# Hymba-style layer on one core: the last row tile first in the routing, two token tiles and three gate units between the embedding's steps

## Chip, core and metric
One core of one Trainium2 chip. The time is the device time of one execution in microseconds (us), as the median of runs. Engines: PE (TensorE), DVE (VectorE), ACT (ScalarE), POOL (GpSimd), SP (SyncE, which here issues most DMAs).

## What is computed
One decoder layer over 1024 tokens of width 1024 in fp32: a mixer (retention and mLSTM heads) with its output projection, a mixture of 32 experts, a gated embedding per layer, and a final norm.
```python
xn = rms_norm(h, attn_norm[l])
h = h + mixer(xn, ...)
xn = rms_norm(h, moe_norm[l])
h = h + hier_moe(xn, ...)      # best group of 4, then 2 of its 8 experts, SwiGLU
...                            # then h gets the gated embedding:
e = rms_norm(p @ w_ple_up, ple_norm)
h = h + sigmoid(rms_norm(h, ple_gate_norm) @ w_ple_gate) * e
```
The routing takes, per token, logits of 4 groups and 32 experts from the normalised row, chooses two experts, sorts the tokens by expert and gathers each expert's rows.

## The kernel before
**Products.** Every large product is three fp32r matmuls (mm3, L216-220): high x high, low x high, high x low. So each operand is split into a high part (a copy on ACT, rounded) and a low part (DVE: value minus high part). Weights come as *units* of 128x2048 (1 MB). The class that streams them has `fetch_to` (SP issues the DMA into a ring of raw buffers as soon as one is free), `split_to` (splits the units up to a number) and `get(u, look)` (gives unit u and splits up to `look` units ahead). Units in `pool_low` have their low part made by POOL (L147), as one 2048-wide operation; units with a scale, as the four of the gate, are split in four pieces by L136 (ACT) and L137 (DVE). A raw buffer is free again when both parts are made.

**Order.** The kernel is scheduled by hand: the order in which the program issues is the order on each engine. Side work is kept in generators that the main loops advance (`pump`, `drain`, `next`).

**Output projection and routing.** Rows are in 8 tiles of 128. `out_half(1, ...)` (L1001 and around) makes rows 512 to 1023 in two column halves. For a finished tile t, `square` (ACT), `norm` (POOL and DVE), `h_trans(t, c)` (4 transposes and a copy to `zT`, by DVE L913 for c = 1), `h_scale` (multiplication L944 and a store into `g_dram`, which the experts gather from) and `last_logits` (4 narrow matmuls L922, then DVE L933 adds the two column halves and L934 scales them) follow. When the last product is done, the kernel drains the side work, issues fetches, then takes the logits of tile 6 (`last_b(6)`), squares, norms and transposes of tile 7 (`last_a(7)`), then tile 7's logits. The routing `route(4)` is a long chain of small DVE operations (from L1247) with a few matmuls (L1263, L1285, L1329) and ends with the gathers of the first experts (POOL L1343). While it runs, units m0+2 and m0+3 (m0: first expert unit) are split with `pool_low`, and m0+4 at the head of `moe`.

**Experts.** A loop over 32 experts: transpose the gathered rows, w1, w3, SiLU, w2; from some expert on one step of the embedding per expert is put between. `gemm2` copies its result, scaled, by ACT (L1394) and scatters it by POOL (L1395) to `Y_dram`. In the last expert's `gemm2`, `look` splits ahead: gate units 0 and 1.

**Branch.** `overflow()` (L1484, L1485) loads a count into every engine and skips a loop that serves experts with too many tokens; in these inputs it is not taken.

**Tail.** The embedding generator `ple` has a step for each tile and column half, here called t2c0 to t7c1 behind the branch: 6 matmuls, a square with a sum by ACT (L1167), and after the second half the reciprocal root on POOL (L1169, L232, L233). In the step c = 0 of tile j the operand of tile j+1 is split (`tps`), and the scaling of tile j-1 (DVE L1146) frees its two accumulators; there are four accumulators. `fill(n)` advances it by n steps; the last `next` only scales tile 7. `add(t)` (DVE L1626, four operations) adds the two experts' rows from `Y_dram`; `trans(t)` (L1635 on) transposes the sum, splits it into `gth` (ACT L236) and `gtl` (DVE L237) and squares it on ACT (L1639). `first(t)` is the gate product of tile t's first column half with gate units 0 and 1, its Sigmoid (ACT L1665, with the load of its function table) and the sums. The second half takes units 2 and 3. From the second row tile on, all tiles repeat one pattern.

Of the kernel before, what the change touches and what calls it, by code (L numbers as in the profile page):

```python
# [10 lines left out]
F32 = mybir.dt.float32  # L11
# [11 lines left out]
P = 128  # L23
# [6 lines left out]
NE = 32  # L30
# [149 lines left out]
class Layer:  # L180
# [674 lines left out]
    def outproj(self):  # L855
# [83 lines left out]
        def h_scale(half, c, n):  # L939

            t, s = half * 4 + n, slice(c * 512, c * 512 + 512)
            hg = post.tile([P, 512], F32, name="hg", bufs=2)
            eng = v if half and c else nc.gpsimd
            eng.tensor_tensor(hg, hb[half, c][:, n], gm[:, s], op=OP.mult)  # L944
            nc.sync.dma_start(self.g_dram[t * P:(t + 1) * P, s], hg)

        def h_store(half, c):
            nc.sync.dma_start(rows(self.h_dram, half, c), hb[half, c])
# [25 lines left out]
        def out_half(half, pumps, before, after):  # L974
            nonlocal y67
            for c in range(2):
                if half == 0 and c == 1:
                    y67 = hold.tile([P, 2, D], F32, name="y67", tag="hb", bufs=3)
                    loaded = {}
                if c:  # L980
                    self.side.append(first_columns(half * 4))
                accs = [psA.tile([P, 512], F32, name="acc") for _ in range(4)]
                _, _, units = self.oplan[half * 2 + c]
                pace = pumps["out%d" % c]
                for ui, u in enumerate(units):
                    H, L = W.get(u, 2 if half and c and ui else 1)
                    for n in range(4):
                        s = slice(n * P, n * P + P)
                        if c == 0 and ui == 0 and n == 0:
                            self.late_last(half * 4)  # L990
                            if half:
                                x_again(1, 0)
                        before(c, ui, n)
                        for kk in range(4):
                            k = ui * 4 + kk
                            self.mm3(accs[n], XH[:, k, s], XL[:, k, s], H[:, kk, :], L[:, kk, :], k == 0, k == KD - 1)
                            if kk == 1:
                                self.pump(pace / 2)
                        if ui == 1:
                            v.tensor_tensor(hb[half, c][:, n], accs[n], hb[half, c][:, n], op=OP.add)  # L1000
                            h_scale(half, c, n)  # L1001
                            if n == 3:
                                h_store(half, c)
                        after(c, ui, n)
                        if half:
                            W.fetch_to(W.nf + 2)
                        if half == 0 and c == 1:
                            j = ui * 4 + n
                            for t in range(4, NT):
                                if t not in loaded and (t, 0) in self.y_done and (t, 1) in self.y_done:  # L1010
                                    self.y_load(t)
                                    loaded[t] = j
                            if j >= 5:
                                self.y_trans(j - 1)
                        self.pump(pace / 2)
                self.mark("out %d %d" % (half, c))
# [17 lines left out]
        def last_a(t):  # L1034
            square(t, 1)
            norm(t)
            h_trans(t, 1)

        last_b = last_logits
        out_half(1, self.PACE[1], none, after)  # L1040
        self.drain()
        self.late_slots = 2
        W.ahead = 99
        W.fetch_to(W.nf + 1)
        last_b(6)
        last_a(7)
        last_b(7)
        ctxP.close()
        pair = self.xp.tile([P, 2 * DX], F32, name="xt", bufs=1)
        nc.gpsimd.memset(pair[:, D:DX], 0.0)  # L1050
# [3 lines left out]
        W.halves = self.m0 + self.HV  # L1054
        W.fetch_to(W.nf + 1)
        next(r)
        W.pool_low = (self.m0 + 2, self.m0 + 3)
        W.split_to(self.m0 + 3)
        for _ in range(4):
            next(r)  # L1060
        for _ in r:
            pass

# [285 lines left out]
    def moe(self):  # L1349
# [52 lines left out]
        hs = {}  # L1402
        blocks = self.overflow_list()
        gather(1)
        W.split_to(self.m0 + 4)
        norm_x(0)
        trans_x(0)
        for e in range(NE + 1):
# [30 lines left out]
        self.tail_open()  # L1439

    def look(self, e, which):
        return 3 if e < self.LK else 2


# [153 lines left out]
    def tail(self):  # L1598
# [21 lines left out]
        def add(t):  # L1620
            h = self.th[t]
            y0, y1 = ty[t]
            for c in range(2):
                for y in (y0, y1):
                    s = slice(c * 512, c * 512 + 512)
                    v.tensor_tensor(h[:, s], h[:, s], y[:, s], op=OP.add)  # L1626

        def trans(t):
            h = self.th[t]
            th = tq.tile([P, KD, P], F32R, name="gth")  # L1630
            tl = tq.tile([P, KD, P], F32R, name="gtl")
            for b in range(2):
                p = psB.tile([P, 4, P], F32, name="pb")
                for k in range(4):
                    nc.tensor.transpose(p[:, k, :], h[:, (4 * b + k) * P:(4 * b + k + 1) * P], self.ident)  # L1635
                self.split_pair(th[:, 4 * b:4 * b + 4], tl[:, 4 * b:4 * b + 4], p)
            gt[t] = (th, tl)
            st = rs[t] = tq.tile([P, 2], F32, name="tst")
            nc.scalar.activation(ty[t][1], h, AF.Square, accum_out=st[:, 0:1])  # L1639
            self.rstd(st[:, 1:2], st[:, 0:1], D)  # L1640
# [45 lines left out]
        def fill(n):  # L1686
            for _ in range(n):
                next(self.ple_gen, None)
# [4 lines left out]
        self.tail_load(1)  # L1693
        load(0)
        load(1)
        fill(9)
        add(0)
        fill(2)
        self.ctxE.close()
        tq = ctxQ.enter_context(tc.tile_pool(name="tq", bufs=2, side="right", reuse_waits="tile"))  # L1700
        self.fn = self.tp.tile([P, D], F32, name="tpt")
        trans(0)
        fill(2)
        add(1)
        self.tail_load(2)
        load(2)
        nc.sync.dma_start(self.fn, bcast_rows(i["final_norm"], D))
# [3 lines left out]
        def first(t, mid=None):  # L1711
            acc = accs[t] = psA.tile([P, 512], F32, name="acc")
            gemm(t, 0, acc, mid=mid)
            finish(t, 0, acc)
# [12 lines left out]
        for t in range(NT):  # L1727
            acc = [None, None]
            if not t:
                first(0, lambda: trans(1))  # L1730
                W.ahead = 99
                W.split_to(len(W.units))
                first(1)
                add(2)
            elif t > 1:
                first(t)
            if t:
                following(t)
            acc[1] = psA.tile([P, 512], F32, name="acc")
            if t < NT - 1:  # L1740
                gemm(t, 1, acc[1])
                finish(t, 1, acc[1])
            else:
                for a, s in ((acc[1], slice(0, 256)), (psA.tile([P, 512], F32, name="acc"), slice(256, 512))):
                    gemm(t, 1, a, s)
                    finish(t, 1, a, s)
            self.mark("gate %d" % t)
            if 2 < t + 2 < NT:
                add(t + 2)
# [52 lines left out]
```

## Time and profile before
| what | value |
|---|---|
| runs | 1323.55 us median of 3 (1320.59 to 1325.12) |
| profiled execution | 1325.77 us, its span 1324.0 us |
| busy | PE 1276.4 us (96%), DVE 948.4 (72%), ACT 787.7 (59%), POOL 289.7 (22%) |
| mean granted TensorE clock | 0.984 |
| stages, us from the span's start | mixer to some 480, projection to 572, routing to 597, experts to 1185, branch to 1189, embedding steps and first additions to 1211, gate to 1324 |

All times in rows are from the start of the span. Matmul rows overlap: the distance of their starts is what one costs. The number in brackets is the idle time of that engine just before, and what released it; "DVEq" is VectorE's sequencer.

### The profile page before, as it was taken

The page shows a single profiled execution, that of the slowest core. Times are in us where ns is not written, and L with a number is a line of the kernel's source. Part 1 is how long each engine was busy: PE and PEld are TensorE (multiplying, and loading weights), DVE is VectorE, ACT ScalarE, POOL GpSimd, SP SyncE. Part 2 cuts the span into 40 slices and gives each one's busy share as a digit, 9 for nine tenths or more (in the row PEclk, how much of TensorE's full clock was granted, in tenths as well). Part 3 has the DMA queues.
Part 4 walks back from the last instruction along what each step waited for, and adds up shares of the span by engine and source line. Part 5 has one row for each costly group of instructions (what it writes and reads, how often), then busy time and mean ns, then how long its engine had stood idle before and what let it go on. Part 6 is the DMA issues. An engine that isn't in the chain of part 4 may idle for free. (4 is left out here: it accounts for less than half of the span.)

```text
span 1324.0 us, 17536 instructions
## 1 busy us (share of the span) xinstructions
PE 1276.4 (96%) x6408; PEld 1061.2 (80%) x6408; DVE 948.4 (72%) x1327; ACT 787.7 (59%) x1154; POOL 289.7 (22%) x364
## 2 busy tenths in 40 slices
PE   7999999999999999959999999999999999988997
PEld 7987888988888888747888888888888887876786
DVE  4557645347773535877999889999999998885665
ACT  5744343434443334336888878888888888774533
POOL 1053112215120442131111121111111231012232
PEclk9999999999999999979999999999999999999999
DMA  9323331332324356857999999999999589956421
GB/s 347 134 98 111 108 121 62 106 110 89 113 88 175 128 212 254 344 202 260 364 387 371 356 376 374 376 368 378 375 375 384 209 358 395 344 191 240 159 96 64
DMA packets 62141, 317.76 MB, mean 240 GB/s; under 512 B 11763, under 2 KB 12339, under 8 KB 32484
## 3 DMA queue, kind: packets, MB, share of 16 engines
q1 hardware_dynamic: 48196, 284.75, 57.4%
q0 software_dynamic: 13712, 31.84, 6.6%
q8 instruction: 51, 0.84, 0.2%
q14 instruction: 38, 0.31, 0.1%
q10 hardware_dynamic: 144, 0.04, 0.0%
HBM read 299.83 MB, written 33.65 MB: 252 GB/s over the span
## 5 line engine op out<-in xcount | busy, mean ns | idle before, releaser
L218 PE MATMUL acc<-wh,XH 128*128 128x512 f32 (+2 forms) x544 | 211.2, 388 | 7.6 <-ACT wh L145 7.2
L219 PE MATMUL acc<-wl,XH 128*128 128x512 f32 (+2 forms) x544 | 203.9, 375 | 1.1 <-DVE wl L147 1.1
L220 PE MATMUL acc<-wh,XL 128*128 128x512 f32 (+2 forms) x544 | 203.9, 375 | 0.3 <-DVE XL L349 0.3
L147 DVE TENSOR_TENSOR wl<-raw,wh 128x1024 fp32r<-128x1024 f32 (+4 forms) x85 | 128.6, 1536 | 77.4 <-ACT wh L145 77.4
L1395 POOL DMA_INDIRECT Y_dram<-y,idx_s x32 | 44.9, 1403 | 471.2 <-ACT y L1394 450.6
L145 ACT ACTIVATE wh<-raw 128x1024 fp32r<-128x1024 f32 (+4 forms) x86 | 110.5, 1314 | 48.3 <-PE acc L220 29.4
L218 PEld LDWEIGHTS acc<-wh,XH 128*128 128x128 f32 x544 | 103.7, 191 | 24.9 <-ACT wh L145 7.4
L220 PEld LDWEIGHTS acc<-wh,XL 128*128 128x128 f32 x544 | 103.5, 190 | 18.2 <-DVE XL L349 0.5
L219 PEld LDWEIGHTS acc<-wl,XH 128*128 128x128 f32 x544 | 103.9, 191 | 17.2 <-DVE wl L147 1.6
L218 PE MATMUL acc<-XH,xth 128*128 128x512 f32 x256 | 104.7, 409 | 0.4 <-ACT xth L236 0.4
L220 PE MATMUL acc<-XH,xtl 128*128 128x512 f32 x256 | 101.5, 396 | 0.3 <-DVE xtl L237 0.3
L219 PE MATMUL acc<-wl,xth 128*128 128x512 f32 x256 | 101.5, 397 | 0.0
L219 PE MATMUL acc<-XL,xth 128*128 128x512 f32 x256 | 101.5, 397 | 0.0
L220 PE MATMUL acc<-wh,xtl 128*128 128x512 f32 x256 | 101.5, 397 | 0.0
L218 PE MATMUL acc<-wh,xth 128*128 128x512 f32 x256 | 101.0, 394 | 0.0
L147 DVE TENSOR_TENSOR XL<-raw,XH 128x1024 fp32r<-128x1024 f32 x58 | 68.3, 1219 | 15.9 <-ACT XH L145 15.9
L147 DVE TENSOR_TENSOR wl<-rawB,wh 128x1024 fp32r<-128x1024 f32 (+1 forms) x61 | 72.9, 1235 | 2.1 <-ACT wh L145 2.1
L147 DVE TENSOR_TENSOR XL<-rawB,XH 128x1024 fp32r<-128x1024 f32 x48 | 56.6, 1218 | 8.4 <-ACT XH L145 8.4
L145 ACT ACTIVATE wh<-rawB 128x1024 fp32r<-128x1024 f32 (+1 forms) x61 | 61.9, 1067 | 0.0
L147 DVE TENSOR_TENSOR XL<-rawH,XH 128x1024 fp32r<-128x1024 f32 x48 | 56.5, 1219 | 7.1 <-ACT XH L145 7.1
L147 DVE TENSOR_TENSOR wl<-rawH,wh 128x1024 fp32r<-128x1024 f32 x48 | 56.5, 1218 | 4.8 <-ACT wh L145 4.8
L220 PEld LDWEIGHTS acc<-XH,xtl 128*128 128x128 f32 x256 | 48.9, 191 | 11.7 <-DVE xtl L237 1.0
(417 smaller groups left out, 3113.5 us busy)
## 6 DMA issues: line engine op xcount, KB each, us to landing
rawB<-in_w SPq DMA_DIRECT2D x56, 1024.0 KB, 8.5
raw<-in_w SPq DMA_DIRECT2D x53, 1024.0 KB, 8.3
rawH<-in_w SPq DMA_DIRECT2D x48, 1024.0 KB, 8.1
hb<-in_w SPq DMA_DIRECT2D x34, 1024.0 KB, 8.4
raw<-in_w_in SPq DMA_DIRECT2D x24, 1024.0 KB, 4.9
raw<-in_w_out SPq DMA_DIRECT2D x8, 1024.0 KB, 5.0
raw<-in_w_in SPq DMA_DIRECT2D x8, 768.0 KB, 6.9
xl<-in_x SPq DMA_DIRECT2D x4, 1024.0 KB, 8.8
```

The source lines that it names most:

```text
L145: self.nc.scalar.activation(h[:, s], r[:, s], AF.Copy)
L147: low.tensor_tensor(l[:, s], r[:, s], h[:, s].bitcast(F32), op=OP.subtract)
L218: self.lastmm = mm(out, lh, rh, start=first, stop=False)
L219: mm(out, lh, rl, start=False, stop=False)
L220: mm(out, ll, rh, start=False, stop=last)
L1395: st = nc.gpsimd.indirect_dma_start(out=self.Y_dram, out_offset=bass.IndirectOffsetOnAxis(ap=self.idx_s[:, e:e + 1], axis=0), in_=y, in_of ...
```

## The change
It has three parts. In the routing, tile 7's copy of transposes, square, norm and row multiplication are issued before the logits of tiles 6 and 7, and the stores behind. The early splits of m0+2 to m0+4 are taken out; these units are now split where the first expert's products ask for them, with DVE for the low parts. And in the tail, gate units 0 and 1 are split between steps of the embedding instead of before the branch, unit 2 before the first gate product; both tiles' additions and transposes stand between the steps, and a Sigmoid of one element, which takes the table load with it, stands behind tile 0's transposes.
```diff
@@ -998,9 +998,10 @@
                                 self.pump(pace / 2)
                         if ui == 1:
                             v.tensor_tensor(hb[half, c][:, n], accs[n], hb[half, c][:, n], op=OP.add)
-                            h_scale(half, c, n)
-                            if n == 3:
-                                h_store(half, c)
+                            if not (half and c and n == 3):
+                                h_scale(half, c, n)
+                                if n == 3:
+                                    h_store(half, c)
                         after(c, ui, n)
                         if half:
                             W.fetch_to(W.nf + 2)
@@ -1038,13 +1039,20 @@
 
         last_b = last_logits
         out_half(1, self.PACE[1], none, after)
+
+        while (7, 0) not in zT:
+            self.pump(1)
+        h_trans(7, 1)
+        square(7, 1)
+        norm(7)
+        h_scale(1, 1, 3)
         self.drain()
+        last_b(6)
+        last_b(7)
+        h_store(1, 1)
         self.late_slots = 2
         W.ahead = 99
         W.fetch_to(W.nf + 1)
-        last_b(6)
-        last_a(7)
-        last_b(7)
         ctxP.close()
         pair = self.xp.tile([P, 2 * DX], F32, name="xt", bufs=1)
         nc.gpsimd.memset(pair[:, D:DX], 0.0)
@@ -1054,10 +1062,6 @@
         W.halves = self.m0 + self.HV
         W.fetch_to(W.nf + 1)
         next(r)
-        W.pool_low = (self.m0 + 2, self.m0 + 3)
-        W.split_to(self.m0 + 3)
-        for _ in range(4):
-            next(r)
         for _ in r:
             pass
 
@@ -1402,7 +1406,6 @@
         hs = {}
         blocks = self.overflow_list()
         gather(1)
-        W.split_to(self.m0 + 4)
         norm_x(0)
         trans_x(0)
         for e in range(NE + 1):
@@ -1439,6 +1442,8 @@
         self.tail_open()
 
     def look(self, e, which):
+        if which == 2 and e == NE - 1:
+            return 0
         return 3 if e < self.LK else 2
 
 
@@ -1693,15 +1698,24 @@
         self.tail_load(1)
         load(0)
         load(1)
-        fill(9)
+        fill(2)
+        W.split_to(self.gate_units[0] + 1)
+        fill(2)
+        W.split_to(self.gate_units[1] + 1)
+        fill(3)
         add(0)
-        fill(2)
+        fill(1)
+        add(1)
+        fill(1)
         self.ctxE.close()
         tq = ctxQ.enter_context(tc.tile_pool(name="tq", bufs=2, side="right", reuse_waits="tile"))
         self.fn = self.tp.tile([P, D], F32, name="tpt")
         trans(0)
-        fill(2)
-        add(1)
+        sg = tq.tile([P, 1], F32, name="sg", bufs=1)
+        nc.scalar.activation(sg, self.ones[:, 0:1], AF.Sigmoid)
+        fill(1)
+        trans(1)
+        fill(3)
         self.tail_load(2)
         load(2)
         nc.sync.dma_start(self.fn, bcast_rows(i["final_norm"], D))
@@ -1727,7 +1741,8 @@
         for t in range(NT):
             acc = [None, None]
             if not t:
-                first(0, lambda: trans(1))
+                W.split_to(self.gate_units[2] + 1)
+                first(0)
                 W.ahead = 99
                 W.split_to(len(W.units))
                 first(1)
```
In the routing, on DVE, from the last addition of the projection to the routing's first reduction. `LG` are logits, `zT` a copied transpose, `hg` the multiplied rows, `zst` the norm's sums. Before:
```order
L933 TENSOR_TENSOR LG<-lg_4658,pb 128x36
L934 SCALAR_TENSOR_TENSOR LG<-LG,zst,bgr 128x36
L899 TENSOR_TENSOR zst<-zst 128x1
L913 COPY zT<-pb 128x512
L928 COPY lg_4658<-pb 128x36 x2
L933 TENSOR_TENSOR LG<-lg_4658,pb 128x36
L934 SCALAR_TENSOR_TENSOR LG<-LG,zst,bgr 128x36
L899 TENSOR_TENSOR zst<-zst 128x1
L913 COPY zT<-pb 128x512
L933 TENSOR_TENSOR LG<-lg_4658,pb 128x36
L934 SCALAR_TENSOR_TENSOR LG<-LG,zst,bgr 128x36
L1247 TENSOR_REDUCE G_4804<-LG 128x16
```
and with the change:
```order
L899 TENSOR_TENSOR zst<-zst 128x1
L913 COPY zT<-pb 128x512
L928 COPY lg_4658<-pb 128x36
L913 COPY zT<-pb 128x512
L899 TENSOR_TENSOR zst<-zst 128x1
L944 TENSOR_TENSOR hg<-hb,gbc 128x512
L928 COPY lg_4658<-pb 128x36
L933 TENSOR_TENSOR LG<-lg_4658,pb 128x36
L934 SCALAR_TENSOR_TENSOR LG<-LG,zst,bgr 128x36
L933 TENSOR_TENSOR LG<-lg_4658,pb 128x36
L934 SCALAR_TENSOR_TENSOR LG<-LG,zst,bgr 128x36
L1251 TENSOR_REDUCE G_4804<-LG 128x16
```
Both pairs of L933 and L934 stand together at the end, behind tile 7's copy and the multiplication.

On POOL at the same place (the gathers are L1343, in the change L1347):
```order
L901 COPY rsc<-zst 128x16
L1050 MEMSET xt 128x16
L1051 MEMSET xt 128x32
L147 TENSOR_TENSOR XL<-rawB,XH 128x2048
L1343 DMA xt<-g_dram,idx_g 128x1040 x2
L147 TENSOR_TENSOR wl<-raw,wh 128x2048
```
and with the change:
```order
L1058 MEMSET xt 128x16
L1059 MEMSET xt 128x32
L1347 DMA xt<-g_dram,idx_g 128x1040 x2
L1368 COPY rx<-xt 128x1
L1347 DMA xt<-g_dram,idx_g 128x1040
L1368 COPY rx<-xt 128x1
```
The two subtractions L147 have gone to DVE, behind the first expert's `xtl`.

On ACT at the branch, whose rows are L1484 and L1485 (L1489 and L1490 in the change), before:
```order
L1394 ACTIVATE y<-pb,gate 128x512 x2
L236 ACTIVATE tps<-tpt 128x256
L1167 ACTIVATE pjunk,pst<-acc 128x512
L136 ACTIVATE XH<-rawB,cols 128x512 x4
L136 ACTIVATE wh<-rawB,cols 128x512 x4
L1394 ACTIVATE y<-pb,gate 128x512 x2
L1484 TENSOR_LOAD trip
L1485 COMPARE_AND_BRANCH x2
```
and with the change:
```order
L236 ACTIVATE hth<-pb 128x512
L145 ACTIVATE wh<-rawB 128x1024 x2
L1398 ACTIVATE y<-pb,gate 128x512 x2
L236 ACTIVATE tps<-tpt 128x256
L1171 ACTIVATE pjunk,pst<-acc 128x512
L1398 ACTIVATE y<-pb,gate 128x512 x2
L1489 TENSOR_LOAD trip
L1490 COMPARE_AND_BRANCH x2
```
The eight splitting copies L136 no longer stand ahead of the copies `y` of the last expert. Behind the branch they stand after the squares `pjunk` of tiles 2 and 3:
```order
L236 ACTIVATE tps<-tpt 128x256
L1171 ACTIVATE pjunk,pst<-acc 128x512 x2
L136 ACTIVATE XH<-rawB,cols 128x512 x4
L236 ACTIVATE tps<-gbc 128x256
L1171 ACTIVATE pjunk,pst<-acc 128x512 x2
L136 ACTIVATE wh<-rawB,cols 128x512 x4
L236 ACTIVATE tps<-gbc 128x256
L1171 ACTIVATE pjunk,pst<-acc 128x512 x2
L236 ACTIVATE tps<-gbc 128x256
L1171 ACTIVATE pjunk,pst<-acc 128x512 x2
```
In the same order, further on, at the first gate tile: `gth` are the copies of transposes, L1644 the square of the tile, `sg` the Sigmoid of one element.
```order
L1171 ACTIVATE pjunk,pst<-acc 128x512
L236 ACTIVATE gth<-pb 128x512 x2
L1644 ACTIVATE raw,tst<-xt 128x1024
L1715 ACT_TABLE_LOAD
L1715 ACTIVATE sg<-cst 128x1
L1171 ACTIVATE pjunk,pst<-acc 128x512
L236 ACTIVATE gth<-pb 128x512 x2
L1644 ACTIVATE rawB,tst<-xt 128x1024
L1171 ACTIVATE pjunk,pst<-acc 128x512 x2
L136 ACTIVATE XH<-rawB,cols 128x512 x4
L1670 ACTIVATE raw<-acc,tst 128x512
```
Before, the row block that answers to it was
```order
L1167 ACTIVATE pjunk,pst<-acc 128x512 x3
L236 ACTIVATE gth<-pb 128x512 x2
L1639 ACTIVATE raw,tst<-xt 128x1024
L1167 ACTIVATE pjunk,pst<-acc 128x512
L236 ACTIVATE gth<-pb 128x512 x2
L1639 ACTIVATE rawB,tst<-xt 128x1024
L1665 ACT_TABLE_LOAD
L1665 ACTIVATE raw<-acc,tst 128x512
L1668 ACTIVATE te_8980,tst_10620<-raw 128x512
L136 ACTIVATE XH<-rawB,cols 128x512 x4
```
The table load moved from behind the first gate product into the space between the two tiles' copies, and the last three squares of the embedding's steps now stand behind it.

## Rows read from the trace of the kernel before
**Rows 1.** Busy time of each engine in stretches, then TensorE's clock, DMA share, GB/s.
```profile
630.00:1000.00 370.00, 370.00 (x1729) 303.23 (x1728) 333.75 (x336) 303.54 (x369) 61.54 (x63) 1.00 0.98 372
...
1218.00:1240.00 22.00, 18.88 (x80) 14.70 (x81) 14.44 (x22) 11.83 (x21) 0.74 (x2) 0.92 0.40 153
1240.00:1312.00 72.00, 72.00 (x338) 58.97 (x338) 44.35 (x67) 28.89 (x60) 23.80 (x39) 1.00 0.28 110
```

**Rows 2.** Timeline (start, us, instruction, idle before) of VectorE, then GpSimd, in the routing.
```profile
574.79 0.25 DVE L934 SCALAR_TENSOR_TENSOR LG<-LG,zst,bgr 128x36 f32<-128x36 f32 x1
...
577.19 3.85 DVE L934 SCALAR_TENSOR_TENSOR LG<-LG,zst,bgr 128x36 f32<-128x36 f32 x1
581.08 0.28 DVE L1247 TENSOR_REDUCE G<-LG 128x16 f32<-128x128 f32 x1
...
576.49 4.50 POOL L147 TENSOR_TENSOR XL<-rawB,XH 128x2048 fp32r<-128x2048 f32 x1
```

**Rows 3.** Timeline of TensorE, last logits to the first expert.
```profile
575.77 1.08 PE L922 MATMUL pb<-wgr,zT 128*128 128x36 f32 x8 [0.85 <-DVE zT L913]
...
585.68 0.48 PE L1263 MATMUL pb<-Mz,onesb 128*128 128x128 bf16 x3 [8.60 <-DVE Mz L1258]
...
597.27 0.79 PE L218 MATMUL acc<-XH,xth 128*128 128x512 f32 x1 [0.17 <-ACT xth L236]
```

**Rows 4.** Timeline: a 2048-wide split on VectorE, and ScalarE before the first expert.
```profile
554.76 2.29 DVE L147 TENSOR_TENSOR XL<-xt,XH 128x2048 fp32r<-128x2048 f32 x1 [3.06 <-ACT XH L145]
...
592.24 1.89 ACT L145 ACTIVATE wh<-raw 128x2048 fp32r<-128x2048 f32 x1
596.62 1.11 ACT L236 ACTIVATE xth<-pb 128x512 fp32r<-128x512 f32 x2 [2.49 <-issue]
```

**Rows 5.** Timeline of TensorE and ScalarE behind and at the branch.
```profile
1189.05 0.76 PE L218 MATMUL acc<-rawHh,tps 128*128 128x512 f32 x1 [3.72 <-DVEq L1485]
...
1191.75 0.56 PE L218 MATMUL acc<-rawHh,tps 128*128 128x512 f32 x1
...
1192.61 0.39 PE L218 MATMUL acc<-rawHh,tps 128*128 128x512 f32 x1
1192.84 0.40 PE L219 MATMUL acc<-rawHl,tps 128*128 128x512 f32 x1
...
1187.53 1.25 ACT L1394 ACTIVATE y<-pb,gate 128x512 f32<-128x512 f32 x2
```

**Rows 6.** Timeline of ScalarE and VectorE: gate splits, an operand's low part, an embedding's scaling.
```profile
1182.62 2.57 ACT L136 ACTIVATE XH<-rawB,cols 128x512 fp32r<-128x512 f32 x4
...
1186.06 2.73 DVE L137 SCALAR_TENSOR_TENSOR wl<-rawB,cols,wh 128x512 fp32r<-128x512 f32 x4
...
1194.59 0.42 DVE L237 TENSOR_TENSOR tps<-gbc,tps 128x256 fp32r<-128x256 f32 x1 [3.40 <-ACT tps L236]
1195.75 1.41 DVE L1146 SCALAR_TENSOR_TENSOR te<-acc,pst,pn 128x512 f32<-128x512 f32 x2 [0.74 <-POOL pst L233]
```

**Rows 7.** Timeline of ScalarE at the first gate product.
```profile
1210.96 1.09 ACT L236 ACTIVATE gth<-pb 128x512 fp32r<-128x512 f32 x2 [2.94 <-PE acc L220]
1211.93 1.06 ACT L1639 ACTIVATE raw<-xt 128x1024 f32<-128x1024 f32 x1
...
1212.97 0.60 ACT L1167 ACTIVATE pjunk<-acc 128x512 bf16<-128x512 f32 x1
...
1224.30 1.28 ACT L1665 ACT_TABLE_LOAD   x1 [2.46 <-PE acc L220]
```

**Rows 8.** List of TensorE's waits (total, times, longest), and two rows of its timeline.
```profile
PE pb L1635 <- DVE xt L1626: 4.6, 4, 3.0
...
PE pb L1635 <- issue: 1.7, 1, 1.7
...
1211.61 0.50 PE L218 MATMUL acc<-XH,gth 128*128 128x512 f32 x1 [0.69 <-ACT gth L236]
...
1239.04 0.47 PE L218 MATMUL acc<-XH,gth 128*128 128x512 f32 x1
```

## Prediction
> **What bounds the kernel now.** I read the stretch table first, then the list of TensorE's waits, then the timelines around each wait. Over the experts TensorE is 100% busy, 370.00 us of 370, with the DMA engines 98% busy, and in the tail after the second row tile's gate product it is 72.00 of 72 [rows 1]: there another order can give nothing. What can move lies between those stretches, in three places. In the routing TensorE waits 8.60 us at 585.68 for VectorE, whose chain of small operations can begin only at 581.08, when the last scaling of the logits is done; that operation took 3.85 us, the same one a tile earlier 0.25 [rows 2, 3]. At the branch around the overflow loop TensorE waits 3.72 us [rows 5]. In the tail it waits 4.6 us for additions ahead of four groups of transposes, 1.7 in front of tile 2's and 0.69 for the gate's first operand [rows 8].
>
> The sum is made against the profiled execution (1325.77 us, span 1324.0). It lies 2.2 us above the median of the runs, 1323.55; I carry the difference over to the median.
>
> **Routing.** The 3.85 us operation starts 0.70 us after GpSimd's 4.50 us subtraction of a 128x2048 weight unit and ends within 0.05 us of its end (577.19 + 3.85 = 581.04; 576.49 + 4.50 = 580.99) [rows 2]. So I read it as 0.25 us of work held up by that subtraction. The change takes both GpSimd subtractions out: -3.6 us. It also puts tile 7's transposes, copy, square and norm ahead of the logits of (7,0) and (6,1). Before, the last logits waited 0.85 us for tile 7's copy and stood alone at 575.77 [rows 3]; now eight matmuls of logits follow back to back on finished copies, and I put the start of the last scaling at 576.05 instead of 577.19 [rows 2], -1.1. Moved past it are the 0.7 us multiplication of the last row block (it already stood ahead of the copy) and on SP three stores; the gather that reads them comes behind the whole routing. VectorE's chain therefore starts 4.7 us earlier, and everything up to the first expert's matmul at 597.27 [rows 3] hangs on it: **-4.7 us**. The stretch stays idle enough that I expect no change in TensorE's clock there.
>
> The two units still have to be split: two ScalarE copies of 1.89 us and two subtractions, on VectorE at 2.29 us as such a unit cost earlier [rows 4]. They come behind the first expert's operands. In the old frame ScalarE is free at about 597.7, so its copies end at 599.6 and 601.5, and VectorE's subtractions, each after its copy, at 601.9 and 604.2. The first expert needs these units after 24 and 36 matmuls: even at 0.233 us each, at 602.9 and 605.7. So they cost nothing; the cover is 1 to 1.5 us. If it is gone, the second expert's operands behind them on VectorE are late next, by up to 1.5 us. One weight buffer is freed some 16 us later (580.99 before, 601.9 - 4.7 now); with TensorE 100% busy from 630 on, no weight was late, so I count nothing.
>
> **The branch.** TensorE's first matmul behind it started 0.27 us after ScalarE had done its scaled copies of the last expert's output (1187.53 + 1.25 = 1188.78) [rows 5], and those stood behind eight splitting copies of gate units 0 and 1 (2.57 us for the first four, the same for the next) [rows 6]. The change moves these splits behind the branch. Then the copies end about 0.65 us after the last expert matmul (1189.05 - 3.72 = 1185.33), near 1186.0, and TensorE starts at 1186.3: a wait of 1.0 for 3.72, **-2.7**. After the old wait six matmuls took 2.70 us (1189.05 to 1191.75), 0.45 each for 0.23 later [rows 5]: the lower of the clock's two levels. With the seventh that is 1.4 us. After 1.0 us I expect none of it, since the 1.7 in front of tile 2's transposes [rows 8] left the clock alone (1.00 from 1240 on [rows 1]): **-1.4**.
>
> **Between the embedding's steps.** Here the splits come back, as waits.
> - The first split's ScalarE part follows the square of step t2c1: 1186.3 + 2.8 (12 matmuls) + 0.9 = 1190.0. VectorE follows 0.7 behind with four operations, 2.73, to 1193.5. Behind them on VectorE wait the operand's low part (0.42) and the embedding's scaling that frees the accumulator for t4c0 (0.70, half of 1.41) [rows 6]. TensorE has used up its 24 matmuls at 1191.95, so it **waits 2.7** and starts at 1194.65.
> - Does the clock fall there? Waits of 3.72 and 3.0 (the longest of the 4.6 [rows 8]; clock 0.92 in its stretch [rows 1]) were followed by the lower level, 1.7 was not. 2.7 is nearest to 3.0: I take it as fallen, 1.3 lost. The other end is no fall.
> - The second split holds t5c0 until 1199.1, fallen or not. Then the rest of the steps waits 0.4 (t6c0), 0.65 and 0.9 (tile 0's two halves, behind the additions), 0.4 and 0.6 (tile 1, and t7c0). The last step, t7c1, ends at 1212.2, where before it ended at 1210.9.
>
> **The first gate product.** ScalarE's copy of tile 0's transposes began at 1210.96, when the last step's matmul had ended, released by that matmul and not by its own transposes [rows 7]: the memory it writes is let go only then. That stays so, and more is now queued behind it on ScalarE. The first gate product needs the accumulator of tile 6's first half, whose scaling on VectorE is behind tile 1's low parts. The chain from 1212.2: two copies 0.97, tile 0's square 1.04, the table load 1.28 and the one-element Sigmoid 0.2, the square of t6c1 0.7, tile 1's two copies 1.0, their last subtraction 0.65, one scaling 0.7, and 0.4 for hand-overs: 6.9 to 7.0 us [rows 6, 7]. TensorE **waits 7.0 us** and starts at 1219.2; before, 1211.61 after 0.69. Then the low clock once more, 1.4 us, in the place of that after the 3.0.
> Against this nothing is left to wait for later: 72 gate matmuls (16.8), tile 2's transposes (0.9, since its addition is long done, so that the 1.7 goes [rows 8]), and the table load is behind. The second column of tile 1 starts at 1219.2 + 1.4 + 16.8 + 0.9 = 1238.3 to 1238.6; before 1239.04 [rows 8]. So branch, steps and gate together give only **-0.5 us**, and -1.8 without the fall at t4c0. All that follows is TensorE at 100% and moves with it.
>
> The Trainium skill (ScalarE: Activation LUTs, What ACT_TABLE_LOAD costs) speaks against the place of the table load: it says that a switch costs a drain of the pipeline too, 2.66 us in all. By that, as an estimate, the wait would be 8.4 us and the sum 1.4 worse. The row at 1224.30 shows 1.28, but it came after a wait of 2.46 [rows 7], where a drain could not be seen.
>
> **Sum:** -4.7 - 0.5 = -5.2: 1320.6 in the profiled frame, **1318.3 us** as a median.
>
> **Rivals.**
> - *TensorE's low clock stays.* From t4c0 on, TensorE meets a wait every 1.4 to 3 us and then one of 7. If the low level held through the steps and the three gate products after them, 41 more step matmuls and 65 more gate matmuls at 0.2 us extra are 21, less 2.3 of waits they would cover: +19, total +13.5, 1337 us. It decides from about 26 further slow matmuls on (26 x 0.2 = 5.2). For it: the waits are closer together than before. Against: after 3.72 us the clock was back within seven matmuls [rows 5], and the 22 us behind the 3.0, with a 1.7 in them, still show 0.92. 0.06.
> - *The weights become the bound.* DMA is 98% busy over 370 us [rows 1]; the buffers set free later could cost what the routing gave, leaving -0.5: 1323. For: the DMA share. Against: TensorE's 100%, with no wait for a weight. 0.08.
> - *The long scaling is not GpSimd's doing*, and VectorE stays held up there. Then the routing gives only 1.1: -1.6, 1322. Against: the two ends agree to 0.05 us, and the one a tile earlier, without such a neighbour, took 0.25. 0.07.
> - *The gate's wait is longer* (a drain at the table load, tile 1's rows of the experts' output landing late, the second expert's operands late): 1.4 to 3 more, total -2 to -4: 1319.6 to 1321.5. 0.16.
>
> **How the numbers follow.** A measurement of this kernel can tell about 0.3%, 4.0 us, from no change. The forecast with either answer on the clock (-4 to -8, so 1315.5 to 1319.5) has 0.63: faster. The weights, the scaling and the longer wait fall within 0.3%, 0.31. The low clock is the slower case, 0.06. The range runs from no fall and a shorter gate chain (-8.5, 1315) to the second and third rival (1322.5).
>
> **What would show it.** In the profile after: the last scaling of the logits at 0.25 us and TensorE's wait before the routing's first count near 5 instead of 8.6; both 2048-wide subtractions on VectorE with no wait of TensorE at 602 to 608; about 1 us at the branch; 2.7 at t4c0; one wait of about 7 us in front of the first gate product, released by VectorE's scaling, and none for the gate's later units or tile 2. A gate wait under 4, or a low clock in the gate product beyond ten matmuls, would make the tail's part wrong; a scaling of over 1 us the routing's.

## The result and the profile after

The changed kernel takes 1317.12 us (median of 7 runs, 1316.09 to 1318.71); the kernel before, beside it, 1324.88 (median of 7, 1320.59 to 1327.5). The ratio is 0.9944, 95% interval 0.9929 to 0.9958: **7.4 us less, between 5.6 and 9.4**. The forecast was 5.2 less and 1318.3 us. The profiled execution of the change took 1318.71 us, its span 1317.1, against 1324.0: 6.9 less.

The routing first, on VectorE (columns as in [rows 2]):

```profile
575.55 0.25 DVE L934 SCALAR_TENSOR_TENSOR LG<-LG,zst,bgr 128x36 f32<-128x36 f32 x1
...
576.45 0.26 DVE L934 SCALAR_TENSOR_TENSOR LG<-LG,zst,bgr 128x36 f32<-128x36 f32 x1
576.74 0.29 DVE L1251 TENSOR_REDUCE G<-LG 128x16 f32<-128x128 f32 x1
```

The scalings of the last two tiles take 0.25 and 0.26 us, and the chain begins at 576.74 instead of 581.08 [rows 2]. Next TensorE, from the routing to the second column of tile 1:

```profile
581.35 0.48 PE L1267 MATMUL pb<-Mz,onesb 128*128 128x128 bf16 x3 [5.01 <-DVE Mz L1262]
...
592.89 0.79 PE L218 MATMUL acc<-XH,xth 128*128 128x512 f32 x1
...
608.10 0.50 PE L220 MATMUL acc<-XH,xtl 128*128 128x512 f32 x1 [0.74 <-DVE xtl L237]
...
1180.28 0.47 PE L218 MATMUL acc<-rawHh,tps 128*128 128x512 f32 x1 [0.30 <-PEq L1490]
...
1188.61 0.47 PE L218 MATMUL acc<-rawHh,tps 128*128 128x512 f32 x1 [2.60 <-DVE te L1150]
...
1189.68 0.63 PE L219 MATMUL acc<-rawHl,tps 128*128 128x512 f32 x1
1190.11 0.63 PE L220 MATMUL acc<-rawHh,tps 128*128 128x512 f32 x1
...
1203.31 0.47 PE L218 MATMUL acc<-rawHh,tps 128*128 128x512 f32 x1 [0.43 <-DVE rawH L1150]
...
1213.17 0.77 PE L218 MATMUL acc<-XH,gth 128*128 128x512 f32 x1 [6.86 <-ACT pjunk L1171]
...
1232.37 0.48 PE L218 MATMUL acc<-XH,gth 128*128 128x512 f32 x1
```

The wait ahead of the routing's first count is 5.01 instead of 8.60 us and the first expert starts at 592.89 instead of 597.27 [rows 3]. At the branch the wait is 0.30, not 3.72 [rows 5], and TensorE's own sequencer ends it. Then come the two waits that the change makes: 2.60 at t4c0 and 6.86 in front of the first gate product, where before it was 0.69 [rows 8]. Before, the wait at t4c0 was 0.46:

```profile
1196.65 0.47 PE L218 MATMUL acc<-rawHh,tps 128*128 128x512 f32 x1 [0.46 <-DVE te L1146]
```

With the change, the distance of the rows at 1189.68 and 1190.11 is 0.43 us, for 0.23 at the full clock. The second column of tile 1 starts at 1232.37 instead of 1239.04 [rows 8]; from there to the end it takes 84.7 us, and before 85.0.

The granted clock of TensorE in two stretches of the change (PEclk, the third number from the end; the second stretch is for the last section):

```profile
1189.50:1191.90 2.40, 2.40 (x8) 1.80 (x7) 2.40 (x5) 2.02 (x5) 0.00 (x0) 0.50 0.97 401
1115.00:1118.00 3.00, 3.00 (x9) 2.27 (x9) 0.54 (x1) 2.20 (x4) 0.36 (x2) 0.53 0.98 367
```

0.50 is the lower of the clock's two levels, 1.2 GHz, here behind the 2.60 us wait.

VectorE, with the two subtractions that GpSimd had, and at the two waits:

```profile
595.48 2.29 DVE L147 TENSOR_TENSOR XL<-rawB,XH 128x2048 fp32r<-128x2048 f32 x1 [1.11 <-ACT XH L145]
597.69 2.28 DVE L147 TENSOR_TENSOR wl<-raw,wh 128x2048 fp32r<-128x2048 f32 x1
...
1187.72 1.40 DVE L1150 SCALAR_TENSOR_TENSOR te<-acc,pst,pn 128x512 f32<-128x512 f32 x2
...
1211.07 1.29 DVE L237 TENSOR_TENSOR gtl<-pb,gth 128x512 fp32r<-128x512 f32 x2 [2.81 <-ACT gth L236]
1212.28 1.40 DVE L1150 SCALAR_TENSOR_TENSOR rawH<-acc,pst,pn 128x512 f32<-128x512 f32 x2
```

And ScalarE, at the branch and at the first gate product:

```profile
1180.02 0.69 ACT L1398 ACTIVATE y<-pb,gate 128x512 f32<-128x512 f32 x1 [0.71 <-PE pb L220]
...
1206.34 1.09 ACT L236 ACTIVATE gth<-pb 128x512 fp32r<-128x512 f32 x2 [7.59 <-PE acc L220]
1207.32 1.06 ACT L1644 ACTIVATE raw<-xt 128x1024 f32<-128x1024 f32 x1
1208.26 0.20 ACT L1644 ACTIVATION_READ_ACCUMULATOR raw<-xt 128x1 f32 x1
1208.48 1.28 ACT L1715 ACT_TABLE_LOAD   x1
1209.78 0.20 ACT L1715 ACTIVATE sg<-cst 128x1 f32<-128x1 f32 x1
1209.88 0.58 ACT L1171 ACTIVATE pjunk<-acc 128x512 bf16<-128x512 f32 x1
...
1210.46 1.07 ACT L236 ACTIVATE gth<-pb 128x512 fp32r<-128x512 f32 x2
```

The copy of tile 0's transposes had 7.59 us of idle time ahead of it (its transposes were done at 1200.3), and the square of t6c1 (1209.88) stands behind square, table load and Sigmoid. The list of waits names a square of ScalarE as what ended the 6.86 us, since that ended at 1213.15. The matmul does not wait for it: it waits for tile 0's copies and for VectorE's scaling that starts at 1212.28, the first half of which is done at 1213.0. It starts 0.89 us after the start of that scaling, just as t4c0 does (1187.72 to 1188.61).

For the experiments the span is cut at three rows of TensorE: the start of the last projection matmul, of the first expert's first matmul, and of the last expert's last one. The part ahead of the first cut runs the same instructions in all kernels here and differs by up to 2.2 us between profiles, so causes are read from the stages and totals from timed runs. The spans are known to 0.1 us, and so is the last stage.

| kernel (one profile each) | routing | experts | from the last expert matmul to the end | span |
|---|---|---|---|---|
| before | 27.59 | 587.66 | 139.07 | 1324.0 |
| the change | 22.78 | 586.69 | 137.52 | 1317.1 |
| routing part alone | 22.40 | 587.51 | 138.98 | 1316.9 |
| no early splits alone | 23.66 | 585.68 | 139.05 | 1317.9 |
| order of the logits alone | 26.52 | 585.01 | 140.00 | 1320.7 |
| tail part alone | 27.50 | 586.14 | 137.52 | 1319.5 |
| change, splits ahead of the branch | 22.69 | 585.11 | 139.11 | 1316.0 |
| change, table load early | 22.30 | 586.72 | 137.12 | 1314.1 |
| change, tile 1 within the product | 22.30 | 586.71 | 138.16 | 1316.6 |
| change, tile 0 in memory of its own | 22.24 | 587.40 | 133.80 | 1312.8 |
| tile 0 behind the steps | 22.41 | 586.70 | 132.67 | 1311.8 |
| and ahead of the last scaling | 22.52 | 586.68 | 129.61 | 1307.0 |
| and one unit split ahead | 22.51 | 585.21 | 128.18 | 1303.9 |

### The profile page after: what moved, and what is told of

It is laid out like the page before. It is cut to its first block, busy times and chain, and to the rows that moved or that the text cites. A ratio compares the mean times of both kernels' runs of the same rounds, so it can differ in the third digit from the quotient of the medians.

```text
span 1317.1 us, 17530 instructions
## 1 busy us (share of the span) xinstructions
PE 1274.1 (97%) x6408; PEld 1062.0 (81%) x6408; DVE 948.3 (72%) x1329; ACT 787.7 (60%) x1155; POOL 278.6 (21%) x362
## 5 line engine op out<-in xcount | busy, mean ns | idle before, releaser
L147 DVE TENSOR_TENSOR wl<-raw,wh 128x1024 fp32r<-128x1024 f32 (+4 forms) x86 | 130.9, 1545 | 79.7 <-ACT wh L145 79.7
L147 DVE TENSOR_TENSOR XL<-raw,XH 128x1024 fp32r<-128x1024 f32 x58 | 68.4, 1221 | 16.3 <-ACT XH L145 16.3
L147 DVE TENSOR_TENSOR wl<-rawB,wh 128x1024 fp32r<-128x1024 f32 (+1 forms) x61 | 72.9, 1236 | 2.0 <-ACT wh L145 2.0
L147 DVE TENSOR_TENSOR XL<-rawB,XH 128x1024 fp32r<-128x1024 f32 (+1 forms) x49 | 58.8, 1241 | 5.8 <-ACT XH L145 5.8
L147 DVE TENSOR_TENSOR XL<-rawH,XH 128x1024 fp32r<-128x1024 f32 x48 | 56.6, 1220 | 6.9 <-ACT XH L145 6.9
L147 DVE TENSOR_TENSOR wl<-rawH,wh 128x1024 fp32r<-128x1024 f32 x48 | 56.5, 1219 | 2.5 <-ACT wh L145 2.5
L145 ACT ACTIVATE XH<-raw 128x1024 fp32r<-128x1024 f32 x58 | 58.1, 1055 | 0.0
```

The lines of the kernel that those rows point to most:

```text
L145: self.nc.scalar.activation(h[:, s], r[:, s], AF.Copy)
L147: low.tensor_tensor(l[:, s], r[:, s], h[:, s].bitcast(F32), op=OP.subtract)
```

## Experiments on the routing

**The routing part alone**, on the kernel before: the hunks of `out_half`, of the order behind it, and the three places that lose `pool_low` and `split_to`; nothing behind the experts.

> The kernel before with the routing part alone (order of tile 7's work and of the logits, no early splits of m0+2 to m0+4); branch and tail as before. My theory: the first expert's matmul starts 4.4 us earlier (592.9 for 597.27), the experts stay at 100%, the last expert matmul starts 5.3 us earlier (1179.6 for 1184.93), and all of it reaches the end: -5.3 us. Rival (the weight stream is the bound, since buffers come free later): the gain is used up within the experts, the last expert matmul stays near 1184.9 and the time within 1 us.

Measured: routing 5.2 us shorter, experts 587.51 us, the rest 138.98 as before; 1320.03 us in 10 runs, ratio 0.9967 (0.9956 to 0.9979), 4.4 us less (2.8 to 5.8). What the routing gives arrives at the end; the weight stream does not take it back.

**Without the early splits, order as before.**
```diff
-        W.pool_low = (self.m0 + 2, self.m0 + 3)
-        W.split_to(self.m0 + 3)
-        for _ in range(4):
-            next(r)
...
-        W.split_to(self.m0 + 4)
```


> The kernel before without the early splits of m0+2 to m0+4 (so without GpSimd's two subtractions), the order of logits and transposes as before. My theory (GpSimd's 4.50 us subtraction holds up VectorE's last scaling of the logits): that scaling takes 0.25 instead of 3.85 us and the first expert's matmul starts 3.3 to 3.8 us earlier (near 593.7). Rival (the scaling waits for something in the order): it still takes 3 to 4 us and the first expert's matmul stays within 1 us of 597.3.

The last scaling of the logits, on VectorE:

```profile
577.02 0.26 DVE L934 SCALAR_TENSOR_TENSOR LG<-LG,zst,bgr 128x36 f32<-128x36 f32 x1
```

0.26 us at the old place in the order; the routing is 3.9 us shorter. The order was not what held it.

**The new order, with the early splits kept** (the hunks of `out_half` and behind it alone).

> The kernel before with the new order of tile 7's work and the logits, but with the early splits on GpSimd. My theory: the subtraction of 4.5 us still runs beside VectorE's chain, and whichever of its operations meets it is held up, the last scaling or one of the next ones with two operands in SBUF; the first expert's matmul starts 0 to 1.2 us earlier than 597.3. Rival (the order alone does it): it starts near 592.9, as with the whole change.

VectorE's last logits and, behind the dots, GpSimd's subtraction:

```profile
575.21 0.19 DVE L933 TENSOR_TENSOR LG<-lg,pb 128x36 f32<-128x36 f32 x1 [0.34 <-PE pb L922]
575.51 4.16 DVE L934 SCALAR_TENSOR_TENSOR LG<-LG,zst,bgr 128x36 f32<-128x36 f32 x1
...
575.12 4.50 POOL L147 TENSOR_TENSOR XL<-rawB,XH 128x2048 fp32r<-128x2048 f32 x1
```

The routing is 1.1 us shorter, no more: the scaling, 1.1 us earlier in the order, now takes 4.16 us, and ends at 579.67, again 0.05 behind GpSimd's operation (575.12 + 4.50 = 579.62). In the run of the tail part alone, in the old order, it met the same subtraction later (576.69, for 575.16), took 3.02 us and ended 0.05 behind it once more: only the end is fixed. Here the addition just ahead of the scaling, at 575.21, ran through in 0.19 us beside the same subtraction; it reads one operand from PSUM, the scaling two from SBUF. That agrees with the Trainium skill (SBUF — State Buffer, Who interferes with whom), by which such a VectorE operation and a GpSimd one that reads SBUF exclude each other for the length of an instruction. 3.9 and 1.1 make up the 4.8 to 5.2 of the whole part.

## Experiments behind the experts

**The tail part alone** (the hunks of `look` and `tail` on the kernel before).

> The kernel before with the part behind the experts alone (no splits of gate units ahead of the branch, splits, additions and transposes between the steps); the routing as before. My theory: from the last expert matmul's start to the end of the span 137.5 us instead of 139.1, so -1.5 us in all, made of -4.9 at the branch (wait 0.3 for 3.7, no low clock) given back by 2.6 with a low clock at t4c0 and 6.9 in front of the first gate product. Rival (the tail gains only because it comes after an earlier routing, by loads landing in time): 0 to +1.

TensorE's waits (total, times, longest):

```profile
PE acc L218 <- ACT pjunk L1167: 6.9, 1, 6.9
PE acc L218 <- DVE te L1146: 2.4, 1, 2.4
...
PE acc L218 <- PEq L1487: 0.4, 1, 0.4
```

137.5 us from the last expert matmul to the end, as with the whole change: some 1.5 less than before, with almost the same waits, whatever the routing does. Timed, in 10 runs: 1321.21 us, ratio 0.9974 (0.9963 to 0.9985), 3.4 us less. With the routing's 4.4 that is 7.8 for the measured 7.4: the parts add up. That the timed tail gives 2 us more than the one profile, just beyond its interval, stays open.

**The splits ahead of the branch again**, all else as changed.
```diff
-        if which == 2 and e == NE - 1:
-            return 0
```


> The changed kernel with gate units 0 and 1 split ahead of the branch again (as before), all else changed. My theory: TensorE waits 3.5 to 3.8 us at the branch instead of 0.3, with the lower clock behind it (1.4), but the 2.6 in front of t4c0 and the lower clock there go; the wait in front of the first gate product stays at 6.9. From the last expert matmul's start to the end of the span 137.5 + 0 to 1.5 us: moving the splits behind the branch is worth 1 us at most. Rival (the splits at the branch cost all of 3.7 + 1.4 and t4c0 waits for something else): 140 to 142.

```profile
PE acc L218 <- ACT pjunk L1171: 6.9, 1, 6.9
...
PE acc L218 <- DVEq L1488: 3.7, 1, 3.7
...
PE acc L218 <- DVE te L1150: 0.2, 1, 0.2
```

The branch costs 3.7 us again, t4c0 0.2, and the gate 6.9: each wait where the theory has it. The whole comes to 139.11, so +1.6 us, a little over the expected 1.5; eleven matmuls of the first gate product ran at the low clock here for eight with the change, 0.6 us of it by their starts.

**The table load ahead of tile 0's transposes.**
```diff
+        sg = self.pst[:, 4 * NT - 1:4 * NT]
+        nc.scalar.activation(sg, self.ones[:, 0:1], AF.Sigmoid)
         self.ctxE.close()
...
         trans(0)
-        sg = tq.tile([P, 1], F32, name="sg", bufs=1)
-        nc.scalar.activation(sg, self.ones[:, 0:1], AF.Sigmoid)
```


> The changed kernel with the one-element Sigmoid, and the table load with it, ahead of tile 0's transposes, where ScalarE is idle. My theory: the load is 1.30 us of the chain in front of the first gate product; the wait there falls from 6.86 to 5.5 and the time by 1.3 us. If a drain belongs to it, by up to 2.7. Rival (the wait hangs on memory or on GpSimd's root and not on ScalarE's queue): it stays at 6.9.

```profile
PE acc L218 <- ACT pjunk L1171: 5.3, 1, 5.3
```

The wait falls by 1.5 us, to 5.35: the load is a link of that chain on ScalarE. But the stage is only 0.4 shorter, for the expected 1.3: thirteen gate matmuls ran at the low clock behind the shorter wait, for eight.

**Tile 1's transposes within the first gate product.**
```diff
-        fill(1)
-        trans(1)
-        fill(3)
+        fill(4)
...
-                first(0)
+                first(0, lambda: trans(1))
```


> The changed kernel with tile 1's transposes within the first gate product, as before the change, in place of between the steps. My theory: VectorE's scaling of tile 6 then follows GpSimd's root and not tile 1's low parts, so the wait in front of the gate falls only from 6.9 to about 6.2, and TensorE's transposes come 0.9 later with no wait: -0.3 to -0.8 us. Rival (tile 1's copies were the wait): 4 or below, -3 us.

A miss on the total: the wait fell as expected, to 6.36, but the stage grew by 0.6 to 138.16. With nothing between t6c1 and t7c0, t7c0 waits 1.6 us for VectorE's scaling instead of 0.43, and ten matmuls were slow for eight. Tile 1's copies were not the main cause of the wait: without them it is only 0.5 shorter.

**Tile 0's copies in memory of their own**, with the tile's sums and the one-element Sigmoid, all in the change's order.
```diff
-            th = tq.tile([P, KD, P], F32R, name="gth")
-            tl = tq.tile([P, KD, P], F32R, name="gtl")
+            if t:
+                th = tq.tile([P, KD, P], F32R, name="gth")
+                tl = tq.tile([P, KD, P], F32R, name="gtl")
+            else:
+                g0 = self.rawB_pool.tile([P, 2048], F32, name="rawB", bufs=3).bitcast(F32R)
+                th, tl = [g0[:, s:s + D].rearrange("p (k n) -> p k n", k=KD) for s in (0, D)]
...
-            st = rs[t] = tq.tile([P, 2], F32, name="tst")
+            st = rs[t] = (tq if t else self.cp).tile([P, 2], F32, name="tst")
...
-        sg = tq.tile([P, 1], F32, name="sg", bufs=1)
+        sg = self.cp.tile([P, 1], F32, name="sg", bufs=1)
```


> The changed kernel in its own order, but tile 0's transposed copies stand in a free weight buffer, and its sums and the one-element Sigmoid in memory of their own, so that none of them has to wait for memory that the last embedding step still reads. My theory: ScalarE copies tile 0 as soon as its transposes are done (a wait of under 1 us in place of 7.59 ahead of the copy), the square, the table load and the square of t6c1 run beside the last step, only tile 1's copies still wait for the memory; the wait in front of the first gate product falls from 6.86 to 2.6 to 3.1 us, and the time by 3.5 to 4.5. Rival (the chain on ScalarE is that long whenever it starts, or the copy waits for something else): 6 or more.

ScalarE's copies of tiles 0 and 1, then TensorE's first gate matmul:

```profile
1198.34 0.60 ACT L236 ACTIVATE rawB<-pb 128x512 fp32r<-128x512 f32 x1 [0.16 <-PE pb L1644]
1199.72 0.60 ACT L236 ACTIVATE rawB<-pb 128x512 fp32r<-128x512 f32 x1 [0.79 <-PE pb L1644]
...
1205.71 1.09 ACT L236 ACTIVATE gth<-pb 128x512 fp32r<-128x512 f32 x2 [2.27 <-PE acc L220]
...
1208.44 0.47 PE L218 MATMUL acc<-XH,rawB 128*128 128x512 f32 x1 [2.76 <-ACT pjunk L1171]
```

This shows the cause. Ahead of tile 0's copies ScalarE idles 0.16 and 0.79 us, released by their own transposes, instead of 7.59 us, released by the last step's matmul; only tile 1's copies still wait (2.27) for that matmul. The wait at the gate is 2.76 and the stage 3.7 us shorter: 4.1 of the 6.86 us are the memory that tile 0's copy waited for at the head of ScalarE's queue.

**Tile 0's transposes behind the steps**, so that the squares of the last steps stand ahead of the copy and not behind it; tile 1's within the product, and without the one-element Sigmoid.
```diff
         add(0)
-        fill(1)
+        fill(2)
         add(1)
-        fill(1)
+        fill(4)
         self.ctxE.close()
...
         trans(0)
-        sg = tq.tile([P, 1], F32, name="sg", bufs=1)
-        nc.scalar.activation(sg, self.ones[:, 0:1], AF.Sigmoid)
-        fill(1)
-        trans(1)
-        fill(3)
...
-                first(0)
+                first(0, lambda: trans(1))
```


> The changed kernel with both additions between the steps but tile 0's transposes behind the last step, and tile 1's within the first gate product; the table load is left to the first Sigmoid. My theory: the 6.9 us come from ScalarE standing with tile 0's copy at the head of its queue until the last step's matmul lets the memory go, with the squares of the last steps behind it. With the copy behind the squares the wait is 1.0 to 1.8 us, its low clock (1.5) goes, and the time falls by 6 to 9 us against the changed kernel, to 1308 to 1311. Rival (VectorE and ScalarE are the bound of this stretch, which only shows at the gate): the waits come back at tile 1's transposes or at units 2 and 3, and the gain is under 3 us.

The first gate matmuls, and VectorE's last scaling and tile 0's low parts:

```profile
1204.17 0.50 PE L218 MATMUL acc<-XH,gth 128*128 128x512 f32 x1 [0.45 <-ACT gth L236]
...
1206.90 0.80 PE L220 MATMUL acc<-XH,gtl 128*128 128x512 f32 x1 [2.00 <-DVE gtl L237]
1207.50 0.63 PE L218 MATMUL acc<-XH,gth 128*128 128x512 f32 x1
...
1204.84 1.41 DVE L1150 SCALAR_TENSOR_TENSOR rawH<-acc,pst,pn 128x512 f32<-128x512 f32 x2 [0.53 <-POOL pst L233]
1206.17 1.28 DVE L237 TENSOR_TENSOR gtl<-pb,gth 128x512 fp32r<-128x512 f32 x2
```

The wait is 0.45 us, below the expected 1.0 to 1.8, and the stage 4.9 us shorter than with the change; timed 1312.79 us, ratio to before 0.9909 (0.9893 to 0.9926). That is less than the expected 6 to 9: t7c0 waits 1.26 us for 0.43, and the third gate matmul now waits 2.00 us, with the low clock behind it. VectorE does the low part behind the scaling of tile 7, since the program puts that into the last step.

**The same, ahead of that last scaling.**
```diff
-        fill(4)
+        fill(3)
         self.ctxE.close()
...
         trans(0)
+        fill(9)
```


> As the run with the transposes behind the steps, but tile 0's transposes are issued ahead of the last scaling of the embedding (tile 7's), so that tile 0's low part does not stand behind it on VectorE. My theory: the 2.00 us that TensorE waited in the first gate product for that low part fall to 0.3 to 0.6, with the low clock behind them (1.5); from the last expert matmul's start to the end of the span 132.7 - 2 to 3.5 = 129 to 130.7, and 2 to 3.5 us less than that run. Rival (the low part was late for another reason, or the scaling now holds up an accumulator): 132 or more.

The 2.00 us and the low clock are gone from the gate product: 129.61, another 3.1 us. Timed 1308.70 us (1308.48 to 1309.2), ratio to before **0.9882** (0.9865 to 0.9898). This beats both kernels, the change by some 8 us.

**And gate unit 0 split ahead of the branch**, unit 1 behind the third step.
```diff
         if which == 2 and e == NE - 1:
-            return 0
+            return 1
...
-        fill(2)
-        W.split_to(self.gate_units[0] + 1)
-        fill(2)
+        fill(3)
         W.split_to(self.gate_units[1] + 1)
-        fill(3)
+        fill(4)
```


> As the run with tile 0's transposes ahead of the last scaling, with gate unit 0 split ahead of the branch again and unit 1 behind the third step. My theory: one unit's copies (2.57 us on ScalarE) end before the last expert's matmul does, so the wait at the branch stays at 1.0 or less, while the 2.5 us at t4c0 fall to 1.8 or less and without the low clock behind it: 1 to 2.5 us less than that run, near 1306 to 1308. Rival (any split ahead of the branch is paid there in full): a wait of 2.5 or more at the branch, no gain.

```profile
PE acc L218 <- DVE te L1150: 2.6, 2, 2.1
...
PE acc L218 <- DVEq L1490: 1.5, 1, 1.5
```

Half a miss: the branch waits 1.5, above the 1.0 expected, and the largest wait in the steps is 2.09, not 1.8, now at t5c0, but without the low clock behind it. The stage is 1.4 shorter. The timed median, 1308.54 (1305.76 to 1311.0), ratio 0.9886 (0.9869 to 0.9904), cannot tell it from the run above.

## Why the prediction came out as it did

The direction and both mechanisms were right; sizes were off. In the two profiles 6.9 us came for the 5.2 of the sum: 0.1 more in the routing, 1.0 in the experts and 1.05 behind them, less 0.4 ahead of the first cut, where the kernels do not differ.

- *Routing, -4.7.* Measured -4.81 in this profile, -5.2 for the part alone, of it 3.9 by GpSimd's subtraction (forecast 3.6) and 1.1 by the order (1.1). The third rival, that the scaling is held by something else, is refuted by the run without the early splits.
- *The two units split late, 0.* No wait for them. The next in the line was late, as named: the second expert's operands, 0.74 us at 608.10, for 0 in the sum and 1.5 as a bound. Before it was 0.31 there (at 612.84), so the change adds 0.4. In the runs with these splits late it goes from 0.28 (routing part alone) to 1.04 (no early splits alone), and is the smaller the more matmuls ran slow at the start of the stage.
- *The experts.* Not in the sum: the stage is 0.97 us shorter. At its start six matmuls ran slow instead of ten, which is 0.7 of it; the later operands take 0.4 back, and the rest is spread over the stage and stays open. Over the runs the number of slow ones goes from four to ten for the same instructions, so I put this gain down to chance and not to the change.
- *The branch, -2.7.* This step failed in size. It had TensorE start 0.27 us behind ScalarE's copies. With the change TensorE started at 1180.28, after 0.30 us of idle time, and ScalarE's last copy ended only at 1180.71: TensorE does not wait for it. Before, VectorE's share of the splits ended at the same time as ScalarE's copies (1186.06 + 2.73 = 1188.79 [rows 6]), and the row named VectorE [rows 5], as it does in both runs with splits ahead of the branch again (3.7 and 1.5 us): I had charged its wait to the wrong of two engines. 0.7 us more gain.
- *t4c0, 2.7 and a fallen clock.* Measured 2.60, fallen, from the fourth matmul on. t6c0 0.40, t7c0 0.43 for 0.4 and 0.6. The fall itself cost almost nothing: t5c0 starts 4.42 us behind t4c0 (1193.03), and 4.30 in the run with tile 0 behind the steps (1188.16 to 1192.46), where the clock fell later and TensorE waited at t5c0. VectorE's second split holds t5c0, as the prediction says ("fallen or not"); its "-1.8 without the fall at t4c0" does not go with that.
- *The first gate product, 7.0.* Measured 6.86, and the chain's links as forecast: copies 0.98, square and sums 1.16, load 1.30, the square of t6c1 0.58. The cause, memory let go by the last step, was read from one row and is shown by the run with memory of its own.
- *Branch, steps and gate, -0.5.* Measured -1.55, the branch's 0.7 being most of the difference; 0.2 lie behind tile 1's second column, and of these the cause stays open.

Of the rivals, the weight stream gave nothing back (the routing part alone keeps its gain), and the low clock lasted 7 matmuls at t4c0 and 8 at the gate, not 106. The Trainium skill's price for the table load (ScalarE: Activation LUTs, What ACT_TABLE_LOAD costs), a drain on top of the load, is not what this row shows: the square's sum ends at 1208.46, the load starts at 1208.48, the Sigmoid at 1209.78. 1.30 us in all, and taking it out shortened the wait by 1.51.

## What to carry to other kernels

A step put early on an in-order engine must be able to run early: look not only for its data but for the memory that it writes, since a copy that waits for a buffer holds the whole queue behind it. When a large share of stalls goes away and the time moves little, look where the same work stands now: here the splits left one wait of 3.7 us and made one of 2.6, and between the last expert matmul and tile 1's second column TensorE idled 12.4 us before and still 11.7 with the change, 6.9 of them in one place. When a wait has two releasers that end together, the price of removing one is known only once the other is placed too.

## What was not expected of the hardware

How long the low clock lasts is not fixed by the wait ahead of it. At the first gate product eight, eight and eleven matmuls were slow behind the same 6.86 us (the change, the tail part alone, the splits ahead of the branch), and thirteen behind 5.35, so that a wait 1.5 us shorter gained 0.4 us. It even comes without a wait. Within the experts stand four matmuls of one row each, 1.98 us in all, with no idle time before or behind them. In nine of the thirteen profiles, the change's among them, the products ran at 0.43 us each from a few matmuls later on, for seven or eight matmuls (first fence, the change); in the other four they stayed at 0.23 (second fence, the run without the early splits, with its granted clock). The granted clock from 1115 to 1118 is 0.53 with the change, as shown above, and 1.00 in that run:

```profile
1111.64 1.98 PE L1159 MATMUL acc<-pn,cst 1*128 1x512 f32 x4
1113.55 0.50 PE L218 MATMUL acc<-rawHh,tps 128*128 128x512 f32 x1
...
1115.13 0.63 PE L220 MATMUL acc<-rawHh,tps 128*128 128x512 f32 x1
1115.56 0.63 PE L218 MATMUL acc<-XH,xth 128*128 128x512 f32 x1
```

```profile
1112.52 1.98 PE L1151 MATMUL acc<-pn,cst 1*128 1x512 f32 x4
1114.43 0.50 PE L218 MATMUL acc<-rawHh,tps 128*128 128x512 f32 x1
...
1115.70 0.39 PE L220 MATMUL acc<-rawHh,tps 128*128 128x512 f32 x1
1115.93 0.39 PE L218 MATMUL acc<-XH,xth 128*128 128x512 f32 x1
...
1115.00:1118.00 3.00, 3.00 (x15) 2.46 (x14) 0.20 (x1) 2.01 (x5) 1.22 (x2) 1.00 0.87 362
```

That is 1.4 us with the same instructions, and nothing in these profiles says which of them get it. With the four to ten slow matmuls at the start of the stage it is most of why the experts' stage reads 585.0 to 587.7 us in the table, and why a single profile should not be asked for differences of 1 us there.
